# A hybrid two-layer expert kernel on one core: small experts' first stages ahead of big second stages, products during the expert choice, and a twelfth weight slot

## Chip, cores and metric

The kernel runs on one core of one Trainium2 chip. The metric is the device time of one execution in microseconds (us), the median of several runs. All data begins and ends in the chip's memory (HBM).

## What is computed

256 latent rows `x` and 256 context rows `ctx`, 1024 wide in float32, go through two layers. Each layer adds a mixer and then a mixture of experts; only the latent rows leave layer 1. The mixer of layer 0 is a pair of gated convolutions, that of layer 1 is attention beside a pooling group; both end in a product with `w_out`. The part that most of the change concerns is the mixture of experts:

```python
    g_logits = (t @ wg + bg).astype(jnp.float32)
    g_idx = jnp.argmax(g_logits, axis=-1)
...
    top_v, top_i = lax.top_k(e_in, TOP_K)
    top_w = jax.nn.softmax(top_v, axis=-1) * g_w
...
    for e in range(N_EXPERTS):
        hid = jax.nn.silu(t @ w1[e]) * (t @ w3[e])
        out = out + gates[:, e:e + 1] * (hid @ w2[e])
```

Each row chooses one of 4 groups and two of that group's 4 experts; an expert goes from 1024 to 512 columns and back. Its input is a modulated RMS norm of the rows, its output is scaled by a modulation row and added to the rows.

## The kernel before

**Engines.** TensorE does the products, ScalarE and VectorE casts and elementwise work, GpSimd gathers and scatters rows, and the queue of SyncE (SP) issues the weight loads. A scheduler fixes each engine's order when the program is built; `tc.issue_after(i)` holds what it encloses behind instruction i in that order, and `tc.high_priority()` moves it forward. An engine works its list strictly in turn.

**Rows.** `X` holds the 512 rows as four chunks of 128 (0 and 1 latent, 2 and 3 context). Layer 1 ends with the two latent chunks.

**Exact products.** `split` (L85) casts each half of a weight tile to a high part `wh` on ScalarE (L93) and subtracts to get a low part `wl` on VectorE (L94); each has NSPL = 4 buffers. `mm3` (L103) then makes a product of three matmuls, at L105, L106 and L107.

**Mixer's end.** `w_out` (L248) is a generator: it goes through two halves of the columns, and in each through two halves of the depth, four chunks and four products each, adding the result to `X` at L274 and L275. `route_prep` (L436) works out what the router's matrix and bias are with norm gain and modulation folded in; its two small products at L461 spread a bias row `bs` over 128 partitions. `router` (L465) transposes the rows (L481), takes the logits (L484), and `dispatch` chooses groups and experts on VectorE up to a mask `M` (L552). Position products (L557, L559) and a selection of the first expert's rows (`select_rows_T`, L723) follow on TensorE.

**Experts.** `experts` (L904) runs all 16 in an order written by hand:

```python
NBIG = (9, 5)
SEQ = ([0, 1, 9, 2, 10, 3, 11, 4, 12, 5, 13, 6, 7, 14, 8, 15],
       [0, 1, 5, 2, 6, 3, 7, 4, 8, 9, 10, 11, 12, 13, 14, 15])
```

The numbers are ranks: 0 and 1 are experts 0 and 1, the others are looked up in a table worked out at the choice (`number`), so that busier experts have lower ranks. Ranks below NBIG are big (128 row places, exact products with split weights: `ffn_in`, `hidden_T`, `down`), the others small (64 places, plain float32 products straight from the loaded weights: `ffn_in_half` at L808, `hidden_half_T` at L821, `down_half` at L834). Each has a first stage (w1 and w3, four loads), a transposed hidden tile, and a second stage (w2, two loads). The loop issues the first stage of expert i with the hidden transposes of i - 1 between its parts, and then `out_e(i - 1)`: the second stage, weighted rows `y` (L942 in layer 0) and a scatter to `Y` in HBM. Where a small expert follows a big one, `early` splits the big one's w2 tiles during the small first stage.

**Weight slots.** Every expert load is 1 MiB. It goes to one of 7 raw tiles (`wr`) or nx = 4 wide ones (`wx`), eleven in turn, and waits on SyncE's queue until the slot's last reader is through. Eleven loads, up to `(wout, 1, 0)`, are issued ahead of the layer's expert loop (`load_ahead`).

**Layer's end.** The last two experts' rows are not scattered but added by products with a selection matrix `selT` (L1075) and, for the scattered ones, products of the identity with rows loaded from `Y` (L1080 in layer 0, L1084 in layer 1). In layer 0 `add_rows` first adds the two halves of each loaded row on VectorE (L1062), and `rows_out(15)` writes the last rows (L873 on ScalarE, L874 on VectorE). Then `X` is updated at L1094 and L1095.

The functions that the diff touches:

Of the kernel before, what the change touches and what calls it, by code (L numbers as in the profile page):

```python
# [19 lines left out]
KD = 8  # L20
# [24 lines left out]
def backbone(ctx: ExitStack, tc: tile.TileContext, I, out):  # L45
# [57 lines left out]
    def mm3(ps, a, b, start, stop):  # L103
# [3 lines left out]
        return T.matmul(ps, a[0], b[1], start=False, stop=stop)  # L107


    X = cp.tile([128, 4, D], F32, name="X")  # L110
    cols = cp.tile([128, NCOL], F32, name="cols")
# [134 lines left out]
    upd = {}  # L246

    def w_out(W, cat, nch, mrows, pool, khs):  # L248

        def load(h, kh):  # L250
            w = raw()
            nc.sync.dma_start(w.rearrange("p (k n) -> p k n", k=4),
                              W[kh * 512:(kh + 1) * 512, h * 512:(h + 1) * 512].rearrange("(k p) n -> p k n", p=128))
            return split(w)

        seq = [(h, n) for h in range(2) for n in range(2)]
        nxt = load(0, khs[0])
        rows = None
        yield
        for i, (h, n) in enumerate(seq):  # L260
            cur, kh = nxt, khs[n]
            if n == 0:
                ps = [pa() for _ in range(nch)]
            for c in range(nch):
                for k in range(4):
                    mm3(ps[c], [t[:, c * 128:(c + 1) * 128] for t in cat(kh * 4 + k)],
                        cur(k * 512, 512), n == 0 and k == 0, n == 1 and k == 3)
                if i < 3 and c == 0:
                    nxt = load(seq[i + 1][0], khs[seq[i + 1][1]])
                if n == 1:  # L270
                    t = pool.tile([128, 512], F32, name="yt", tag="tmp", bufs=4)
                    if not rows:
                        rows = mrows()
                    V.tensor_tensor(t, ps[c], rows[c // 2][:, h * 512:(h + 1) * 512], op=ALU.mult)  # L274
                    upd[c] = V.tensor_tensor(X[:, c, h * 512:(h + 1) * 512], X[:, c, h * 512:(h + 1) * 512], t, op=ALU.add)  # L275
            yield


    def even_layer():
        with tc.tile_pool(name="ev", bufs=1, reuse_waits="tile") as ep:  # L280
# [147 lines left out]
            while rest:  # L428
                mod_chunk(*rest.pop(0))
            prep = route_prep(0, 2, Ar, Br, ep.tile([128, 2, KD, 32], F32, name="wa", tag="bp"))  # L430
            for _ in wo:
# [4 lines left out]
    def route_prep(l, nr, Ar, Br, wa):  # L436
# [22 lines left out]
        V.tensor_copy(bs[:, 0:nr], pb[0:32, 0, 0:nr])  # L459
        for r in range(nr):  # L460
            T.matmul(pb[:, 2 + r, :], bs[:, r:r + 1].to_broadcast([32, 128]), ident[0:32, 0:32], start=True, stop=True)  # L461
            V.tensor_tensor(bw[:, r, :], pb[:, 2 + r, 0:20], bge[:, l, :], op=ALU.add)
        return Ar, Br, wa, bw

    def router(l, nch, prep):  # L465
# [33 lines left out]
        with tc.high_priority():  # L499
            lgT = sp.tile([128, 128], F32, name="lgT")  # L500
            i = V.tensor_copy(lgT[:32 * nch, :], pl[:32 * nch, :])
            with tc.issue_after(i.ins):
                rows(nch - 1)
            pl2 = py((128, 128))
            T.transpose(pl2[:, :32 * nch], lgT[:32 * nch, :], ident[:32 * nch, :32 * nch])

# [3 lines left out]
    def dispatch(l, nch, nr, pl2, rs, bw, hmD, hms, ir):  # L510
# [44 lines left out]
        for c in range(nch + 1):  # L555
            for cc in range(c):
                T.matmul(pr[:, c], ones_b, M[:, cc], start=cc == 0, stop=c == nch and cc == c - 1)  # L557
            if c < nch:
                T.matmul(pr[:, c], tri, M[:, c], start=c == 0, stop=True)  # L559

# [168 lines left out]
    loaded = []  # L729

    def behind(i):
# [68 lines left out]
    def ffn_in_half(x, loads, hs, between=()):  # L800

        ps = [pa((128, 256)), pa((128, 256))]
        for kh in range(2):
            for m in range(2):
                w = loads.pop(0)()
                for k in range(4):
                    for h in range(2):
                        T.matmul(ps[m][64 * h:64 * h + 64, :], x[:, k, kh * 64:kh * 64 + 64], w[:, k * 512 + h * 256:k * 512 + h * 256 + 256],  # L808
                                 start=kh == 0 and k == 0, stop=kh == 1 and k == 3)
                for f in between[:1]:  # L810
                    f()
                between = between[1:]
# [91 lines left out]
    def experts(l, R, after, mid=None):  # L904
# [3 lines left out]
        with tc.tile_pool(name=f"mp{l}", bufs=1, reuse_waits="tile") as mp:  # L908
# [39 lines left out]
            def out_e(i):  # L948
                rows_out(i, (down_half if small[i] else down)(hT.pop(i), wout[i]))

            win, wout, hs, hT = {}, {}, {}, {}
            nx = 4
            turn = [0]

            def slot():
# [3 lines left out]
                if 2 <= i < NRAW + 2:  # L959
                    return raw()  # L960
                return wide(i % NRAW, [128, 2048])

# [14 lines left out]

            load_ahead([(win, 0, i) for i in range(4)] + [(win, 1, i) for i in range(4)] + [(wout, 0, i) for i in range(2)] + [(wout, 1, 0)])
            if l == 0:
# [75 lines left out]
            def add_rows(c):  # L1055
# [5 lines left out]
                else:  # L1061
                    V.tensor_tensor(y[:, :D], y[:, :D], y[:, D:], op=ALU.add)  # L1062

            for c in range(nch):
                add_rows(c)
            rows_out(NE - 1, po)
            for r in range(R.nr):
# [82 lines left out]
    def odd_layer(A, B):  # L1150
        with tc.tile_pool(name="od", bufs=1, reuse_waits="tile") as op:
# [188 lines left out]
            next(wo)  # L1340
            prep = route_prep(1, 1, ABr[:, 0:1, :], ABr[:, 1:2, :], tmp((128, 2, KD, 32)))
            for _ in wo:
# [119 lines left out]
```

## Time and profile before

| | |
|---|---|
| three runs | 1006.71, 1008.33, 1011.28 us; median 1008.33 |
| profiled execution, its own time | 1006.41 us |
| its span, first to last instruction | 1004.6 us |
| mean granted TensorE clock | 0.966 |
| TensorE busy with matmuls | 915.2 us (91%) |
| VectorE, ScalarE, GpSimd busy | 595.0, 393.7, 124.1 us |
| DMA | 313.66 MB, mean 312 GB/s over the span |
| layer 0: mixer and w_out, choice, experts, end | 0 to 269, to 286, to about 540, to 580 us |
| layer 1: mixer and w_out, choice, experts, finish | 580 to 729, to 742, to 983, to 1004.6 us |

How to read it: the engines run side by side, so their busy times do not add up to the span. What counts is, stage by stage, which wait ends last. A row of the timeline is start, duration, engine, source line, operation, result <- operands, count, and in brackets how long the engine stood before it and on what. A granted clock of 1.00 is TensorE at 2.4 GHz, 0.50 is 1.2 GHz. A float32 matmul appears as two records; `L105`, `L93` and the like are lines of the listing above.

### The profile page before, as it was taken

What the parts mean: (1) busy time and instruction counts of PE and PEld (TensorE: products, weight loads), DVE (VectorE), ACT (ScalarE), POOL (GpSimd) and SP (SyncE); (2) the same over time, 40 slices, a digit from 0 to 9 for tenths busy, and PEclk for the clock granted to TensorE, in tenths of its full rate; (3) what the DMA queues carried; (4) which work ended last, traced back from release to release, by engine and by line L of the source; (5) the groups of instructions that cost most, each with busy time, mean ns of one, the idle gap of its engine ahead of it and who ended that gap; (6) DMA issues with size and microseconds to landing.
All of it is one profiled execution on the core that took longest, in us unless ns stands there. A gap on an engine that the chain in (4) does not pass through costs nothing. (4 is left out here: it accounts for less than half of the span.)

```text
span 1004.6 us, 13295 instructions
## 1 busy us (share of the span) xinstructions
PE 915.2 (91%) x4893; PEld 615.4 (61%) x4893; DVE 595.0 (59%) x942; ACT 393.7 (39%) x571; POOL 124.1 (12%) x127
## 2 busy tenths in 40 slices
PE   2799999999799999999999889999978999999875
PEld 0466776557587776666666368655766766655431
DVE  2689999354778744446544577675587755520004
ACT  2432211321447655445544147433356544411102
POOL 3000000040112111111001011010021211111000
PEclk9899999998999999999999989999978999999999
DMA  9998888993578999999996663253368999999994
GB/s 358 353 335 299 309 320 314 361 343 135 205 307 327 411 407 420 419 399 397 383 355 222 216 226 133 99 191 122 121 227 321 375 388 418 419 418 418 418 419 180
DMA packets 80680, 313.66 MB, mean 312 GB/s; under 512 B 8602, under 2 KB 32154, under 8 KB 50016
## 3 DMA queue, kind: packets, MB, share of 16 engines
q1 hardware_dynamic: 70032, 290.34, 75.0%
q0 software_dynamic: 6368, 11.78, 3.2%
q10 hardware_dynamic: 4208, 10.61, 2.8%
q8 instruction: 40, 0.66, 0.3%
q14 instruction: 32, 0.26, 0.1%
HBM read 301.56 MB, written 21.23 MB: 321 GB/s over the span
## 5 line engine op out<-in xcount | busy, mean ns | idle before, releaser
L93 ACT CAST wh<-wr 128x1024 fp32r<-128x1024 f32 (+2 forms) x170 | 172.0, 1037 | 151.1 <-PE pa L107 50.9
L94 DVE TENSOR_TENSOR wl<-wr,wh 128x1024 fp32r<-128x1024 f32 (+2 forms) x170 | 199.4, 1203 | 53.7 <-ACT wh L93 52.4
L105 PE MATMUL pa<-wh,xh 128*128 128x512 f32 x224 | 93.4, 417 | 6.8 <-ACT wh L93 5.0
L107 PE MATMUL pa<-wl,xh 128*128 128x512 f32 x224 | 91.5, 409 | 2.2 <-DVE wl L94 2.1
L808 PE MATMUL pa<-wr,xs 128*64 128x256 f32 x736 | 88.1, 384 | 4.5 <-DMA wr<-in_moe_w 4.5
L106 PE MATMUL pa<-wh,xl 128*128 128x512 f32 x224 | 90.6, 405 | 0.9 <-DVE xl L712 0.9
L334 DVE SCALAR_TENSOR_TENSOR ca<-apad,cols,ca 128x512 f32<-128x512 f32 x120 | 84.0, 746 | 0.8
L808 PEld LDWEIGHTS pa<-wr,xs 128*64 128x64 f32 x736 | 49.6, 136 | 37.0 <-DMA wr<-in_moe_w 8.2
L105 PE MATMUL pa<-wx,wh 128*128 128x512 f32 x160 | 63.6, 402 | 4.0 <-ACT wx L234 4.0
L106 PE MATMUL pa<-wx,wl 128*128 128x512 f32 x160 | 62.7, 393 | 0.0
L107 PE MATMUL pa<-wx,wh 128*128 128x512 f32 x160 | 62.5, 392 | 0.0
L183 PE MATMUL py<-wr,csil 128*32 128x512 f32 x384 | 51.3, 638 | 11.0 <-ACT csil L154 11.0
L94 DVE TENSOR_TENSOR wl<-wx,wh 128x1024 fp32r<-128x1024 f32 x46 | 54.7, 1221 | 7.0 <-ACT wh L93 5.9
L105 PEld LDWEIGHTS pa<-wh,xh 128*128 128x128 f32 x224 | 43.8, 196 | 17.2 <-ACT wh L93 6.3
L93 ACT CAST wh<-wx 128x1024 fp32r<-128x1024 f32 x46 | 47.0, 1052 | 17.8 <-DVE M L552 6.7
L107 PEld LDWEIGHTS pa<-wl,xh 128*128 128x128 f32 x224 | 43.5, 194 | 14.8 <-DVE wl L94 4.7
L808 PE MATMUL pa<-wx,xs 128*64 128x256 f32 x416 | 49.0, 382 | 2.2 <-DMA wx<-in_moe_w 2.2
L106 PEld LDWEIGHTS pa<-wh,xl 128*128 128x128 f32 x224 | 43.4, 194 | 10.5 <-DVE xl L712 1.2
L815 DVE TENSOR_TENSOR hs<-hs,pa 128x256 f32<-128x256 f32 x18 | 7.6, 422 | 67.9 <-PE pa L808 67.9
L105 PE MATMUL py<-wh,hTh 128*128 128x512 f32 x112 | 46.0, 410 | 1.5 <-ACT wh L93 1.5
L107 PE MATMUL py<-wl,hTh 128*128 128x512 f32 x112 | 44.4, 415 | 2.6 <-DVE wl L94 2.3
L106 PE MATMUL py<-wh,hTl 128*128 128x512 f32 x112 | 44.3, 396 | 0.0
(360 smaller groups left out, 1526.1 us busy)
## 6 DMA issues: line engine op xcount, KB each, us to landing
wr<-in_moe_w SPq DMA_DIRECT2D x124, 1024.0 KB, 12.3
wx<-in_moe_w SPq DMA_DIRECT2D x68, 1024.0 KB, 10.4
wr<-in_w_mod SPq DMA_DIRECT2D x48, 1024.0 KB, 8.5
wr<-in_ev_w_in SPq DMA_DIRECT2D x20, 512.0 KB, 5.9
wr<-Y SPq DMA_DIRECT2D x6, 1024.0 KB, 6.0
wr<-in_ev_w_out SPq DMA_DIRECT2D x4, 1024.0 KB, 5.1
Y<-xg SPq DMA_DIRECT2D x1, 4096.0 KB, 13.3
wr<-in_od_w_out SPq DMA_DIRECT2D x4, 1024.0 KB, 5.1
```

What stands on the lines that cost most here:

```text
L93: S.copy(hi[:, :m], x)
L94: V.tensor_tensor(lo[:, :m], x, hi[:, :m].bitcast(F32), op=ALU.subtract)
L105: T.matmul(ps, a[0], b[0], start=start, stop=False)
L106: T.matmul(ps, a[1], b[0], start=False, stop=False)
L107: return T.matmul(ps, a[0], b[1], start=False, stop=stop)
L183: T.matmul(ps[32 * j:32 * j + 32, :], csil[:, l, k, :], w[:, j * 512:(j + 1) * 512], start=k == 0, stop=k == 7)
L334: V.scalar_tensor_tensor(acc, apad[:, bi, :, t:t + 256], col("caw", t * 4 + bi), acc, op0=ALU.mult, op1=ALU.add)
L808: T.matmul(ps[m][64 * h:64 * h + 64, :], x[:, k, kh * 64:kh * 64 + 64], w[:, k * 512 + h * 256:k * 512 + h * 256 + 256], start=kh == 0 and ...
L815: V.tensor_tensor(hs, hs, ps[1], op=ALU.mult)
```

## The change

It does six things.

1. `route_prep` returns its two bias products as a function `later`. Both layers call it after one more step of `w_out`, behind the last product issued so far (`done[0]`).
2. `awake(i, n)` issues n products of the identity with the router's weights `wge` (128x512) behind an instruction i. Their result is not read. Five (layer 0) or four (layer 1) stand behind the transpose of the logits, one behind the position products.
3. `out_e` issues the second stage of i behind the last first-stage product of i + 1 where expert i + 1 is small (`done[0]`, now also set in `ffn_in_half`).
4. In layer 0 `rows_out(15)` stands behind the last of `add_rows`.
5. `X` becomes two tiles, `xl` (latent) and `xc` (context), with the same index as before.
6. In layer 1 nx is 5: the twelfth slot is the tile `xc`, and one more load, `(wout, 1, 1)`, is issued ahead.

```diff
@@ -106,8 +106,23 @@
         return T.matmul(ps, a[0], b[1], start=False, stop=stop)

-
-    X = cp.tile([128, 4, D], F32, name="X")
+    def awake(i, n):
+
+        with tc.issue_after(i.ins):
+            ps = pa()
+            for _ in range(n):
+                T.matmul(ps, ident, wge.rearrange("p l k n -> p (l k n)"), start=True, stop=True)
+
+
+    class Rows:
+
+        def __init__(self):
+            self.t = [cp.tile([128, 2, D], F32, name=n, tag=n) for n in ("xl", "xc")]
+
+        def __getitem__(self, at):
+            return self.t[at[1] // 2][at[0], at[1] % 2, at[2]]
+
+    X = Rows()
     cols = cp.tile([128, NCOL], F32, name="cols")
     nc.scalar.dma_start(cols, I.cols)
@@ -245,6 +260,8 @@
     upd = {}

+    done = [None]
+
     def w_out(W, cat, nch, mrows, pool, khs):

@@ -263,8 +280,8 @@
             for c in range(nch):
                 for k in range(4):
-                    mm3(ps[c], [t[:, c * 128:(c + 1) * 128] for t in cat(kh * 4 + k)],
-                        cur(k * 512, 512), n == 0 and k == 0, n == 1 and k == 3)
+                    done[0] = mm3(ps[c], [t[:, c * 128:(c + 1) * 128] for t in cat(kh * 4 + k)],
+                                  cur(k * 512, 512), n == 0 and k == 0, n == 1 and k == 3)
                 if i < 3 and c == 0:
                     nxt = load(seq[i + 1][0], khs[seq[i + 1][1]])
@@ -427,7 +444,9 @@
             while rest:
                 mod_chunk(*rest.pop(0))
-            prep = route_prep(0, 2, Ar, Br, ep.tile([128, 2, KD, 32], F32, name="wa", tag="bp"))
+            prep, later = route_prep(0, 2, Ar, Br, ep.tile([128, 2, KD, 32], F32, name="wa", tag="bp"))
+            next(wo)
+            later()
             for _ in wo:
                 pass
@@ -457,10 +476,14 @@
         bs = sp.tile([32, 2], F32, name="bs")
         V.tensor_copy(bs[:, 0:nr], pb[0:32, 0, 0:nr])
-        for r in range(nr):
-            T.matmul(pb[:, 2 + r, :], bs[:, r:r + 1].to_broadcast([32, 128]), ident[0:32, 0:32], start=True, stop=True)
-            V.tensor_tensor(bw[:, r, :], pb[:, 2 + r, 0:20], bge[:, l, :], op=ALU.add)
-        return Ar, Br, wa, bw
+
+        def later():
+            with tc.issue_after(done[0].ins):
+                for r in range(nr):
+                    T.matmul(pb[:, 2 + r, :], bs[:, r:r + 1].to_broadcast([32, 128]), ident[0:32, 0:32], start=True, stop=True)
+                    V.tensor_tensor(bw[:, r, :], pb[:, 2 + r, 0:20], bge[:, l, :], op=ALU.add)
+
+        return (Ar, Br, wa, bw), later

     def router(l, nch, prep):
@@ -502,7 +525,7 @@
                 rows(nch - 1)
             pl2 = py((128, 128))
-            T.transpose(pl2[:, :32 * nch], lgT[:32 * nch, :], ident[:32 * nch, :32 * nch])
+            awake(T.transpose(pl2[:, :32 * nch], lgT[:32 * nch, :], ident[:32 * nch, :32 * nch]), 5 - l)

         with tc.high_priority():
@@ -554,9 +577,10 @@
         for c in range(nch + 1):
             for cc in range(c):
-                T.matmul(pr[:, c], ones_b, M[:, cc], start=cc == 0, stop=c == nch and cc == c - 1)
+                i = T.matmul(pr[:, c], ones_b, M[:, cc], start=cc == 0, stop=c == nch and cc == c - 1)
             if c < nch:
-                T.matmul(pr[:, c], tri, M[:, c], start=c == 0, stop=True)
+                i = T.matmul(pr[:, c], tri, M[:, c], start=c == 0, stop=True)
+        awake(i, 1)

         R.pe = cp.tile([128, nch, 16], F32, name=f"pe{l}", tag="pe")
@@ -805,8 +828,8 @@
                 for k in range(4):
                     for h in range(2):
-                        T.matmul(ps[m][64 * h:64 * h + 64, :], x[:, k, kh * 64:kh * 64 + 64], w[:, k * 512 + h * 256:k * 512 + h * 256 + 256],
-                                 start=kh == 0 and k == 0, stop=kh == 1 and k == 3)
+                        done[0] = T.matmul(ps[m][64 * h:64 * h + 64, :], x[:, k, kh * 64:kh * 64 + 64], w[:, k * 512 + h * 256:k * 512 + h * 256 + 256],
+                                           start=kh == 0 and k == 0, stop=kh == 1 and k == 3)
                 for f in between[:1]:
                     f()
@@ -946,10 +969,13 @@

             def out_e(i):
-                rows_out(i, (down_half if small[i] else down)(hT.pop(i), wout[i]))
+
+                with behind(done[0]) if small[i + 1] else nullcontext():
+                    po = (down_half if small[i] else down)(hT.pop(i), wout[i])
+                rows_out(i, po)

             win, wout, hs, hT = {}, {}, {}, {}
-            nx = 4
+            nx = 4 + l
             turn = [0]

@@ -958,6 +984,9 @@
                 if 2 <= i < NRAW + 2:
                     return raw()
+                if i == NRAW + 4:
+
+                    return cp.tile([128, 2048], F32, name="xc", tag="xc")
                 return wide(i % NRAW, [128, 2048])

@@ -975,7 +1004,7 @@
                     d[e][i] = lambda w=w: w

-            load_ahead([(win, 0, i) for i in range(4)] + [(win, 1, i) for i in range(4)] + [(wout, 0, i) for i in range(2)] + [(wout, 1, 0)])
+            load_ahead([(win, 0, i) for i in range(4)] + [(win, 1, i) for i in range(4)] + [(wout, 0, i) for i in range(2)] + [(wout, 1, 0)] + [(wout, 1, 1)] * l)
             if l == 0:
                 clear(nc.sync, 0, XG[0])
@@ -1059,11 +1088,13 @@
                         V.tensor_tensor(X[:, c, :], X[:, c, :], y[:, h * D:(h + 1) * D], op=ALU.add)
                 else:
-                    V.tensor_tensor(y[:, :D], y[:, :D], y[:, D:], op=ALU.add)
+                    i = V.tensor_tensor(y[:, :D], y[:, :D], y[:, D:], op=ALU.add)
+                    return i

             for c in range(nch):
-                add_rows(c)
-            rows_out(NE - 1, po)
+                i = add_rows(c)
+            with nullcontext() if l else tc.issue_after(i.ins):
+                rows_out(NE - 1, po)
             for r in range(R.nr):
                 cs = (2 * r, 2 * r + 1)
@@ -1338,7 +1369,9 @@
             wo = w_out(I.od_w_out, lambda k: (ch[:, k, :], cl[:, k, :]), 2, lambda: [m2], op, (1, 0))
             next(wo)
-            prep = route_prep(1, 1, ABr[:, 0:1, :], ABr[:, 1:2, :], tmp((128, 2, KD, 32)))
+            prep, later = route_prep(1, 1, ABr[:, 0:1, :], ABr[:, 1:2, :], tmp((128, 2, KD, 32)))
+            next(wo)
+            later()
             for _ in wo:
                 pass
             return router(1, 2, prep)

```

Three places show how the order moves. Line numbers behind the diff's first lines are shifted (L461 becomes L483, L481 L504, L808 L831, L821 L844, L874 L897, L1062 L1091, L1094 L1125).

TensorE, layer 0, in the middle of `w_out` (`pa`: the product's sum, `ah` and `al`: its rows, `bs`: the bias row), before and then after:

```order
L106 MATMUL pa<-wh,al 128x512
L461 MATMUL pt<-ident,bs 128x32
L107 MATMUL pa<-wl,ah 128x512
L105 MATMUL pa<-wh,ah 128x512
L106 MATMUL pa<-wh,al 128x512
L107 MATMUL pa<-wl,ah 128x512
L105 MATMUL pa<-wh,ah 128x512
L461 MATMUL pt<-ident,bs 128x32
L106 MATMUL pa<-wh,al 128x512
L107 MATMUL pa<-wl,ah 128x512
```

```order
L107 MATMUL pa<-wl,ah 128x512
L105 MATMUL pa<-wh,ah 128x512
L106 MATMUL pa<-wh,al 128x512
L504 MATMUL pt<-ident,xl 128x128 x4
L107 MATMUL pa<-wl,ah 128x512
L483 MATMUL pt<-ident,bs 128x32
L105 MATMUL pa<-wh,wx 128x512
L106 MATMUL pa<-wh,wx 128x512
L107 MATMUL pa<-wl,wx 128x512
```

The two products on `bs` stood among the products of the first column half, and the transposes of X behind those; now the transposes come first, one product ahead of the half's end, and the `bs` products stand behind them, the second 12 products further on.

TensorE, layer 0, the fourth pair of a big expert and a small one behind it (`hTh`, `hTl`: the big expert's hidden tile, second stage; `xs`: the small one's rows, first stage; `xh`, `xl`: rows of the next big expert), before and then after:

```order
L107 MATMUL py<-wl,hTh 128x512 x2
L105 MATMUL py<-wh,hTh 128x512
L106 MATMUL py<-wh,hTl 128x512
L808 MATMUL pa<-wr,xs 64x256 x8
L107 MATMUL py<-wl,hTh 128x512
L105 MATMUL py<-wh,hTh 128x512
L106 MATMUL py<-wh,hTl 128x512
L107 MATMUL py<-wl,hTh 128x512
L821 MATMUL pt<-ident,hs 128x128 x2
L699 MATMUL pt<-ident,xg_1961 128x128 x4
L105 MATMUL pa<-wh,xh 128x512
L106 MATMUL pa<-wh,xl 128x512
```

```order
L831 MATMUL pa<-wr,xs 64x256 x8
L802 MATMUL pt<-ident,hs 128x128 x4
L733 MATMUL pt<-ident,xg_1971 128x128 x3
L831 MATMUL pa<-wr,xs 64x256 x8
L733 MATMUL pt<-ident,xg_1971 128x128 x5
L831 MATMUL pa<-wr,xs 64x256 x16
L105 MATMUL py<-wh,hTh 128x512
L106 MATMUL py<-wh,hTl 128x512
L107 MATMUL py<-wl,hTh 128x512
```

Before, the last eight products of the small first stage stand among the second-stage products, the hidden transposes (L821) and those of the gathered rows (L699) next, and the next big expert's first products behind them. After, the whole small first stage stands ahead of all 24 second-stage products; the hidden transposes (L844) come 12 products into the next big expert.

VectorE, end of layer 0 (`xl` at L874 and L897 is the low part of expert 14's rows, `ya` that of expert 15's, `wr` a chunk of the rows loaded from Y, `zt` a scaled sum), before and then after:

```order
L874 SCALAR_TENSOR_TENSOR xl<-py,gate_2095,xh 128x512 x2
L874 SCALAR_TENSOR_TENSOR ya<-py,gate_2095,ya 128x512
L1062 TENSOR_TENSOR wr<-wr 128x1024 x2
L1094 TENSOR_TENSOR zt<-pa,wr 128x512 x2
L1095 TENSOR_TENSOR X<-X,zt 128x512 x2
L1062 TENSOR_TENSOR wr<-wr 128x1024
L1094 TENSOR_TENSOR zt<-pa,wr 128x512
L159 TENSOR_SCALAR rsqm<-ss1b 128x1
L1094 TENSOR_TENSOR zt<-pa,wr 128x512
L223 TENSOR_SCALAR scr<-X,rs1b 128x1024
L1062 TENSOR_TENSOR wr<-wr 128x1024
L1095 TENSOR_TENSOR X<-X,zt 128x512 x2
```

```order
L897 SCALAR_TENSOR_TENSOR xl<-py,gate_2104,xh 128x512 x2
L1091 TENSOR_TENSOR wr<-wr 128x1024 x4
L897 SCALAR_TENSOR_TENSOR ya<-py,gate_2104,ya 128x512
L1125 TENSOR_TENSOR zt<-pa,wr 128x512 x2
L1126 TENSOR_TENSOR xl<-xl,zt 128x512 x2
L1125 TENSOR_TENSOR zt<-pa,wr 128x512 x2
L174 TENSOR_SCALAR rsqm<-ss1b 128x1
```

Before, the last expert's rows stand ahead of all four additions, and two of the additions stand between updates of X. After, all four come first.

## Rows read from the trace of the kernel before

**Rows 1.** Chain of waits, 900 to 1005 us: start us, us, what.
```profile
913.39 6.93 PE pa L808 x64
...
962.93 20.09 DMA wr<-in_moe_w
...
983.16 1.94 PE py L834 x8
```

**Rows 2.** Stretches: length; busy PE, PEld, DVE, ACT, POOL; PEclk, DMA share, GB/s.
```profile
430.00:530.00 100.00, 92.45 (x449) 62.41 (x448) 55.71 (x55) 56.16 (x72) 11.68 (x10) 0.97 0.98 381
...
825.00:985.00 160.00, 148.02 (x951) 86.66 (x949) 46.26 (x54) 38.36 (x57) 21.79 (x19) 1.00 1.01 417
```

**Rows 3.** Timeline of TensorE, w_out of layer 0: start us, us, instruction [idle before].
```profile
225.38 0.40 PE L461 MATMUL pt<-ident,bs 32*128 32x32 f32 x2 [2.24 <-DVE bs L459]
...
230.05 0.63 PE L106 MATMUL pa<-wh,al 128*128 128x512 f32 x1
230.48 0.63 PE L107 MATMUL pa<-wl,ah 128*128 128x512 f32 x1
...
233.57 0.39 PE L107 MATMUL pa<-wl,ah 128*128 128x512 f32 x1
233.80 0.60 PE L481 MATMUL pt<-ident,X 128*128 128x128 f32 x4
```

**Rows 4.** Timeline of VectorE, w_out of layer 0.
```profile
225.25 1.20 DVE L94 TENSOR_TENSOR wl<-wr,wh 128x1024 fp32r<-128x1024 f32 x1
...
228.81 1.28 DVE L274 TENSOR_TENSOR yt<-pa,wr 128x512 f32<-128x512 f32 x2
230.00 1.28 DVE L275 TENSOR_TENSOR X<-X,yt 128x512 f32<-128x512 f32 x2
```

**Rows 5.** Timeline of TensorE: choice of layer 0, of layer 1, and the end.
```profile
275.28 0.19 PE L559 MATMUL py<-M,tri 128*128 128x16 bf16 x1 [5.64 <-DVE M L552]
...
276.86 9.12 PE L723 MATMUL pt<-scr 128*128 128x128 f32 x64 [1.04 <-DVE scr L566]
...
734.17 0.20 PE L559 MATMUL py<-M,tri 128*128 128x16 bf16 x1 [4.91 <-DVE M L552]
...
735.22 6.70 PE L723 MATMUL pt<-scr 128*128 128x128 f32 x32 [0.74 <-DVE scr L566]
...
991.75 3.70 PE L1084 MATMUL pa<-wr,ident 128*128 128x512 f32 x8 [0.34 <-DMA wr<-Y]
```

**Rows 6.** Stretches at the two choices, columns as in rows 2.
```profile
277.00:280.50 3.50, 3.50 (x17) 3.50 (x18) 3.50 (x18) 0.32 (x2) 0.00 (x0) 0.51 1.01 406
735.00:741.00 6.00, 5.78 (x27) 5.78 (x28) 5.27 (x17) 3.17 (x7) 2.79 (x2) 0.50 0.33 138
741.00:744.00 3.00, 3.00 (x17) 2.60 (x17) 1.90 (x12) 2.02 (x3) 0.00 (x0) 0.96 0.37 87
```

**Rows 7.** Waits of TensorE, 425 to 560 us: total us, times, longest.
```profile
PE pa L105 <- ACT wh L93: 4.4, 4, 1.7
PE py L107 <- DVE wl L94: 2.3, 1, 2.3
PE pa L107 <- DVE wl L94: 2.1, 4, 0.5
PE py L105 <- ACT wh L93: 1.2, 4, 0.3
```

**Rows 8.** Waits of TensorE, 290 to 425 us.
```profile
PE py L105 <- ACT wh L93: 0.3, 1, 0.3
```

**Rows 9.** Timeline of ScalarE, 420 to 440 us.
```profile
429.65 1.40 ACT L942 ACTIVATE y<-py,gate 128x512 f32<-128x512 f32 x2 [3.90 <-PE py L107]
```

**Rows 10.** Timelines of VectorE, then TensorE, end of layer 0.
```profile
565.76 0.75 DVE L874 SCALAR_TENSOR_TENSOR ya<-py,gate,ya 128x512 fp32r<-128x512 f32 x1 [5.40 <-ACT ya L873]
566.43 2.35 DVE L1062 TENSOR_TENSOR wr<-wr 128x1024 f32<-128x1024 f32 x2
...
567.70 1.98 PE L1080 MATMUL pa<-wr,ident 128*128 128x512 f32 x4 [2.04 <-DVE wr L1062]
```

## Prediction

> **What bounds the kernel now.** I read the chain of waits first, from its end. Its last long steps are weight loads, the last of them 20.09 us from issue to landing with others in flight, and TensorE's next products begin where it lands [rows 1]. The table by stretches says why: from 825 to 985 us the DMA engines are busy throughout at 417 GB/s, while TensorE works for 148 of 160 us [rows 2]. So the end of layer 1 is set by how many loads are still to come, and by when the slots for them came free. From 430 to 530 us, in layer 0, the DMA engines look almost as busy (0.98), but their rate is 381 GB/s. The waits of TensorE from 425 to 560 us name the casts of the split weights, ScalarE's high halves and VectorE's low ones, and no DMA [rows 2, 7]. So there time is lost in TensorE's own chain. Whatever shortens that chain ahead of 825 us frees slots earlier and moves the later loads with it. Three more places of that chain are waits around the router and the layer's end; each has its part below.
>
> **Constant products of the route.** In layer 0 TensorE stands 2.24 us for the bias row bs before the two products at L461, then runs at half clock (1.2 of 2.4 GHz): its products start 0.43 us apart (230.05, 230.48), later 0.23 (233.57, 233.80) [rows 3]. The change sends 18 products ahead of that point and the constant products behind them. TensorE is free at 225.38 - 2.24 = 223.14; 19 products at 0.23 bring it to 227.5. There the transposes of X wait in turn: VectorE still does two low halves at 1.20, two yt products in 1.28 and the first of two X additions at 0.64 [rows 4], from 225.25 to 229.6. They start there and not at 233.80, 4.2 us earlier. But 2.1 us of that is a new wait, nearly as long as the old one, and the old one cost much of the clock: 225.38 to 233.80 is 8.42 us for 19 products, which at 0.23 take 4.4; of the 4.0 more I put 1.0 on the constant products themselves and 3.0 on the clock. If the new wait costs as much, 1.2 is left; if nothing, 4.2. I take **2.2**: the clock falls, but shorter, since the wait is. In layer 1 I found no wait at this product: nothing.
>
> **Products that keep TensorE awake.** At the choice TensorE stands 5.64 us in layer 0 and 4.91 in layer 1 [rows 5], and the select products that follow begin at half clock (0.51 in layer 0 until 280.5, 0.50 in layer 1 until 741) [rows 6]. The change puts 5 and 4 products of the 128x128 identity with 512 columns there. The same form at L1084 takes 3.70 us for 8 records, which are 4 instructions: 0.925 us each [rows 5]. That is 4.6 us in a wait of 5.64, and 3.7 in one of 4.91, so they end 1 us early and cost nothing. One more follows the position products, 0.925 in waits of 1.04 and 0.74, so 0.2 late in layer 1. If the clock holds, the stretch from 276.86 to 280.5 halves: 1.8 us. VectorE, busy for all of 277 to 280.5 with the choice's own work [rows 6], caps that; I take **1.5** of 0 to 1.8. In layer 1 about 6 us at half clock would give 3.0, but VectorE's idle time is only 0.73 + 1.10 us there [rows 6]; I take **1.8** of 0 to 3.0 (nothing, if the clock falls anyway).
>
> **Second stages behind the next first stage.** In layer 0 the big expert's down products alternate with the next, small expert's first stage from the fourth such pair on. Behind them ScalarE has two weighted rows of 0.70 us [rows 9] and a hidden copy ahead of the next big expert's casts, and TensorE waits for those casts. The change puts the small first stage ahead, so that the big down products cover what ScalarE owes. Of the waits in rows 7, 4.4 + 2.1 + 2.3 + 1.2 = 10.0 us, two (2.2 together: the longest of 1.7 and one of 0.5 behind it) fall between two big experts and stay. At most 7.8 us go, at four transitions; one in layer 1 changes too. Nothing less than zero is to be expected of the new order alone: the first three transitions already have it, and from 290 to 425 us the casts of weights cost TensorE 0.3 us in all [rows 8]. The DMA engines limit the gain: 100 us at 381 GB/s would be 91 at 417 [rows 2], 9 us of room, but not at every transition. I take **6.0** of 0 to 7.8. What the old order covered, and the new doesn't, is a late load of the small first stage: the down products stood between its parts (third rival).
>
> **Last rows behind the additions.** At layer 0's end VectorE stands 5.40 us for ScalarE's last row (L873), and only then adds the Y halves at L1062, two of which take 2.35. TensorE waits 2.04 for them [rows 10]. Behind the change all four additions run inside the 5.40 us (4.7, if Y has landed), so the 2.04 goes, and the third and fourth, 1.18 each, leave the X chain. That is 2.0 to 4.4; I take **3.5**, since the odd layer's start also waits for other things.
>
> **A twelfth slot.** X is split, so the context's half can take one MiB load in layer 1. It is issued on SyncE's queue behind the band load, with nothing to wait for but the last reader of the context's rows. One load fewer is left for the saturated stretch: 1.0486 MB at 417 GB/s [rows 2], **2.5** us, all of it on the path, as TensorE has 12 us of slack there. The Trainium skill, "DMA: Bandwidth & Descriptors", section "Specifications", gives about 358 GB/s as a core's HBM limit. By that the load would be worth 2.9 us and the sum 0.4 more; the row shows 417, so the measurement stands.
>
> **Sum.** 2.2 + 1.5 + 1.8 + 6.0 + 3.5 + 2.5 = 17.5 us off the profiled execution's 1006.41, so 988.9. The median of the three runs, 1008.33, is 1.9 above that execution, so **990.8 us**. All lower ends (1.2, 0, 0, 0, 2.0, 2.5) give 5.7 us and 1002.6; all upper ends (4.2, 1.8, 3.0, 7.8, 4.4, 2.5) 23.7 and 984.6.
>
> **Rivals.**
> First, the load stream already binds in layer 0: the 6.0 of the second stages is absorbed, and the new wait at the transposes costs the full half clock. What is left is 1.2 + 1.5 + 1.8 + 3.5 + 2.5 = 10.5, so 997.8. For it speaks the share near 1 there, against it that no wait there names a DMA [rows 2, 7].
> Second, the clock falls at the choice all the same: the products end about 1 us before the mask, and single short waits remain. Then 3.3 us are lost: 994.1. For it: a wait of 2.24 us was enough to lose the clock in rows 3; against it, no gap here is that long. The Trainium skill, "TensorE: Matmul & The Clock Gate", section "A second HAM failure mode: psum-queue depth-cycling", tells of short idle gaps between groups that make the clock oscillate; no run here shows it at this place.
> Third, slower: at the five changed transitions the small first stage now stands whole ahead of the down products, and its four loads are late. TensorE runs such a stage in 6.93 us [rows 1], four loads at 2.5 us are 10.0, so it waits 3.1 where the down products, 24 at 0.23 or 5.5 us, used to fill in, and the clock falls (up to 3.0 as above, middle 1.5): 4.6. Five are 23.0, against 11.5 from the other parts: 11.5 slower, **1019.8**. It decides from the third such transition on. Against it: no wait in rows 7 names a DMA, so the loads are ahead there, by up to eleven slots.
> Fourth, the twelfth slot does nothing, because its load waits for the context's last reader and delays the loads queued behind it: 2.5 lost, 993.3. Against it: the loads near 600 us are few.
>
> **How the numbers follow.** Forecast 0.52, first rival 0.18, second 0.14, fourth 0.10, third 0.06. The range of 8 in 10 runs from 984 to 1002, about the two ends of the sum: it holds the first, second and fourth rival, and leaves out the third and misses that add up. 0.5% is 5 us, about what a measurement here can tell from no change, so faster means under 1003.3. The forecast and the three mild rivals lie there, 0.94, less 0.06 for misses that add up: 0.88. Slower by over 0.5% is the third rival, less a little: 0.05. The rest, 0.07, is the same.
>
> **What would show it.** In layer 0 the 2.24 us wait at the constant products is gone, and the first transposes of X wait about 2 us and start 4 us earlier against the w_out stage's beginning. The select products take about 7.3 and 4 us (9.12 and 6.70 before [rows 5]) at a granted clock of 1.0. The sum of cast waits between 425 and 545 us falls from 10 to some 2 to 4. The 2.04 us wait at L1080, now L1111, is gone. The last weight load lands about 16 us earlier, and the stretch before it still shows a DMA share near 1. I'd be wrong if waits for loads of 2 us or more stand at the small first stages of layer 0, if the choice still shows 0.50, or if the last load lands less than 8 us earlier although TensorE reaches layer 1 earlier.

## The result and the profile after

The changed kernel took 991.33 us (988.52 to 993.46, 4 runs) against 1008.96 beside it: ratio 0.9841, 95% interval 0.9818 to 0.9863. The forecast was 990.8. Two later measurements of the same kernel gave 0.9810 (0.9779 to 0.9840) and 0.9811 (0.9786 to 0.9835).

The page of the changed kernel's profiled execution (988.52 us), as against a span of 1004.6 us before:

```profile
span 986.8 us, 13346 instructions
...
PE 910.4 (92%) x4915; PEld 615.9 (62%) x4915; DVE 595.9 (60%) x942; ACT 393.7 (40%) x571; POOL 122.0 (12%) x127
```

TensorE is busy 4.8 us less than the 915.2 before, although eleven awake products of 0.925 us came in.

The chain of waits at its end, then the stretch from 800 us (length; busy PE, PEld, DVE, ACT, POOL; PEclk, DMA share, GB/s):

```profile
944.11 20.07 DMA wx<-in_moe_w
...
964.31 1.94 PE py L857 x8
```

```profile
800.00:965.00 165.00, 154.36 (x994) 92.56 (x992) 48.80 (x57) 41.59 (x61) 23.52 (x20) 1.00 1.01 418
```

The last load still ends the chain [rows 1], in a stream as full as before [rows 2], and lands 18.8 us earlier (944.11 + 20.07 = 964.18, against 983.02). So what happened ahead of it was passed on. Where it happened shows when layer 0's late part is cut at the starts of the small experts' second stages (L834, now L857). The work between two starts is the same, as the counts show. Before, then after, in the columns above:

```profile
410.11:446.05 35.94, 33.78 (x172) 21.81 (x171) 17.35 (x17) 17.10 (x22) 4.82 (x4) 0.95 1.01 412
446.05:480.79 34.74, 33.33 (x176) 21.22 (x175) 16.99 (x17) 16.46 (x21) 4.84 (x4) 1.00 1.00 392
480.79:537.46 56.67, 52.33 (x251) 36.11 (x250) 33.73 (x33) 32.48 (x41) 4.07 (x4) 0.97 0.94 358
537.46:560.29 22.83, 19.99 (x114) 10.93 (x113) 8.50 (x11) 6.96 (x10) 3.80 (x5) 1.00 0.51 183
```

```profile
412.38:442.70 30.32, 30.32 (x172) 21.26 (x171) 16.99 (x17) 16.93 (x22) 4.81 (x4) 1.00 1.02 420
442.70:473.49 30.79, 30.79 (x176) 21.74 (x175) 17.08 (x17) 16.41 (x21) 4.35 (x4) 1.00 1.01 419
473.49:523.26 49.77, 48.68 (x251) 35.51 (x250) 33.46 (x33) 32.11 (x41) 4.79 (x4) 1.00 1.01 413
523.26:544.86 21.60, 18.70 (x114) 11.36 (x113) 8.40 (x12) 7.06 (x10) 3.79 (x5) 1.00 0.71 280
```

The four stretches together went from 150.18 to 132.48 us: 17.70 less, as much as the whole gain (they start 2.3 us later, and what follows them is 2.4 us shorter). 6.76 of it are waits (stretch less busy PE: 10.75 before, 3.99 after). The other 10.94 are TensorE's own busy time for the same instructions. Part of that is the clock, at 0.95 and 0.97 in the first and third stretch before, 1.00 after; by the granted clocks of their slices of 2 us, an estimate, it cost 3.4 us. The larger part is not the clock: in the second and fourth stretch the clock was 1.00 both times, and still the busy time fell by 2.54 and 1.29. Taken apart by the starts of its products, with the waits taken off, the second stretch became shorter by 1.1 us in the 24 second-stage products, by 0.9 in the transposes of the gathered rows, and by 0.7 in the small experts' products and the hidden transposes; the next big expert's 48 first-stage products took 11.5 us both times.

TensorE's waits for casts from 425 to 560 us, 10.0 in rows 7, are now these (total us, times, longest):

```profile
PE py L107 <- DVE wl L94: 2.7, 1, 2.7
PE pa L105 <- ACT wh L93: 0.6, 1, 0.6
...
PE pa L107 <- DVE wl L94: 0.5, 1, 0.5
```

That is 3.8. The one long wait for low halves stayed, 2.3 before and 2.7 now; of the two that were to stay (2.2) half went.

The places of the other parts. The constant products, TensorE's timeline:

```profile
231.83 0.63 PE L504 MATMUL pt<-ident,xl 128*128 128x128 f32 x4 [1.73 <-DVE xl L292]
...
232.62 0.40 PE L483 MATMUL pt<-ident,bs 32*128 32x32 f32 x2
```

The old wait of 2.24 is gone and the new one is 1.73 [rows 3]. The clock stays at 1.00 here.

The choice, layer 0 and then layer 1:

```profile
268.87 4.46 PE L114 MATMUL pa<-wge,ident 128*128 128x512 f32 x10
274.68 0.18 PE L582 MATMUL py<-M,tri 128*128 128x16 bf16 x1 [1.35 <-DVE M L575]
...
276.24 7.41 PE L747 MATMUL pt<-scr 128*128 128x128 f32 x64
283.40 0.48 PE L105 MATMUL pa<-wh,xh 128*128 128x512 f32 x1
```

```profile
713.25 3.70 PE L114 MATMUL pa<-wge,ident 128*128 128x512 f32 x8
718.23 0.18 PE L582 MATMUL py<-M,tri 128*128 128x16 bf16 x1 [1.28 <-DVE M L575]
...
719.31 3.79 PE L747 MATMUL pt<-scr 128*128 128x128 f32 x32
```

The awake products (L114) fill the waits of 5.64 and 4.91 up to 1.35 and 1.28, and the select products take 7.41 and 3.79 us for 9.12 and 6.70 [rows 5]. In this profile that part does, up to here, what was forecast. In the changed kernel's two later profiles the clock fell at layer 0's choice all the same. The same stretch there, 276 to 278 us, in the first profile and then in the second:

```profile
276.00:278.00 2.00, 1.92 (x16) 1.77 (x16) 2.00 (x10) 0.32 (x2) 0.00 (x0) 1.00 1.02 410
```

```profile
276.00:278.00 2.00, 2.00 (x11) 2.00 (x11) 2.00 (x10) 0.00 (x0) 0.00 (x0) 0.50 1.02 410
```

The end of layer 0:

```profile
549.71 3.60 PE L1111 MATMUL pa<-wr,ident 128*128 128x512 f32 x8
...
564.53 0.69 PE L1147 MATMUL pt<-ident,scr 128*128 128x128 f32 x2 [2.64 <-DVE scr L238]
```

The products on the rows from Y start without a wait, where 2.04 stood [rows 10], but the second transposes of layer 1, the odd layer, now wait 2.64 us for VectorE, where they waited 0.51 before.

### The profile page after: what moved, and what is told of

Its sections match the earlier page's. It is cut to its first block, busy times and chain, and to the rows that moved or that the text cites. A ratio compares the mean times of both kernels' runs of the same rounds, so it can differ in the third digit from the quotient of the medians.

```text
span 986.8 us, 13346 instructions
## 1 busy us (share of the span) xinstructions
PE 910.4 (92%) x4915; PEld 615.9 (62%) x4915; DVE 595.9 (60%) x942; ACT 393.7 (40%) x571; POOL 122.0 (12%) x127
## 5 line engine op out<-in xcount | busy, mean ns | idle before, releaser
L94 DVE TENSOR_TENSOR wl<-wr,wh 128x1024 fp32r<-128x1024 f32 (+2 forms) x168 | 197.2, 1204 | 42.7 <-ACT wh L93 41.2
L831 PE MATMUL pa<-wr,xs 128*64 128x256 f32 x640 | 75.6, 383 | 4.0 <-DMA wr<-in_moe_w 4.0
L831 PEld LDWEIGHTS pa<-wr,xs 128*64 128x64 f32 x640 | 43.7, 137 | 30.8 <-DMA wr<-in_moe_w 7.9
L831 PE MATMUL pa<-wx,xs 128*64 128x256 f32 x416 | 49.5, 382 | 1.8 <-DMA wx<-in_moe_w 1.8
L105 PE MATMUL pa<-wh,wx 128*128 128x512 f32 (+1 forms) x112 | 42.8, 384 | 0.5 <-ACT wh L93 0.5
```

The source lines that it names most:

```text
L94: V.tensor_tensor(lo[:, :m], x, hi[:, :m].bitcast(F32), op=ALU.subtract)
L105: T.matmul(ps, a[0], b[0], start=start, stop=False)
L831: done[0] = T.matmul(ps[m][64 * h:64 * h + 64, :], x[:, k, kh * 64:kh * 64 + 64], w[:, k * 512 + h * 256:k * 512 + h * 256 + 256], start=k ...
```

## The experiments

Each ratio is against the kernel before, measured beside it on the same chip; the changed kernel itself came out at 0.984, 0.981 and 0.981 in three measurements.

**The second stages alone.** Every other part is taken back, except that X stays two tiles and that in layer 1 the constant products keep their new place:

```diff
-            with nullcontext() if l else tc.issue_after(i.ins):
+            with nullcontext():
                 rows_out(NE - 1, po)
-            nx = 4 + l
+            nx = 4
...
-            next(wo)
-            later()
+            later(False)
...
-            awake(T.transpose(...), 5 - l)
+            awake(T.transpose(...), 0)
...
-        awake(i, 1)
```

> Only the second stages are moved behind the next first stage; the constant products, the awake products, the order at layer 0's end and the eleven slots are as before (X stays split in two tiles). Theory: this part is most of the change. In the two traces the five late transitions of layer 0 took 5.6, 4.0, 2.8, 4.1 and 1.2 us less, 17.7 together, so this kernel is 13 to 18 us faster than before, 991 to 996. Rival, the size in my prediction: 6 us, about 1003.

Measured 991.91 us, 0.9855 (0.9823 to 0.9887): 14.6 us off by the ratio. This part is most of the change. The split of X was not tried by itself. The constant products of layer 1 gain nothing: from its first router product to the logits' transpose it is 29.3 to 29.4 us in the profile before and in all the others.

**All but the second stages.**

```diff
-                with behind(done[0]) if small[i + 1] else nullcontext():
+                with nullcontext():
                     po = (down_half if small[i] else down)(hT.pop(i), wout[i])
```

> The changed kernel with the second stages issued where they were before. Theory: it loses nearly the whole gain, 1004 to 1009. Rival, the size in my prediction: 6 us are lost, about 997. In both cases the waits for casts between 425 and 560 us should be back, some 8 to 10 us.

Measured 1004.72 us, 0.9978 (0.9955 to 1.0001). The other five parts together are worth some 2 us, between none and 4.5 by the interval, where the forecast had 11.5. The waits of TensorE from 400 to 560 us (total us, times, longest), of this kernel and then of the one with the second stages alone:

```profile
PE pa L105 <- ACT wh L93: 4.4, 4, 1.7
PE py L105 <- ACT wh L93: 2.8, 5, 1.6
PE pa L107 <- DVE wl L94: 2.1, 4, 0.5
PE py L107 <- DVE wl L94: 2.1, 1, 2.1
```

```profile
PE py L107 <- DVE wl L94: 2.2, 1, 2.2
PE pa L105 <- ACT wh L93: 0.6, 1, 0.6
PE pa L107 <- DVE wl L94: 0.5, 1, 0.5
```

The cast waits are back with the old order, 11.4 us in all (one of 1.6 ahead of 425 us), and 3.3 without it.

**Layer 0's awake products left out, twice, and both layers'.**

```diff
-            awake(T.transpose(...), 5 - l)
+            awake(T.transpose(...), 4 * l)
...
-        awake(i, 1)
+        if l:
+            awake(i, 1)
```

> The changed kernel without the six awake products of layer 0. Theory: TensorE comes 2.3 us earlier out of the choice with them, but stands for the gathered rows of the second expert until 300 us all the same, and loses the clock in that longer wait; without them the select products take 9.1 us again and the kernel is 0 to 2.5 us faster, 989 to 991.5. Rival, the size in my prediction: 1.5 us slower, 993.

> Layer 0's awake products left out, a second time, now beside the changed kernel. Theory: what they gain at the choice (1.5 us) is given back behind it, since the earlier start meets waits for the second expert's rows and casts (1.39 and 0.93 us for 0.44 and 0.87) that cost the clock: the same or up to 2 us faster than the changed kernel. Rival, the size in my prediction: 1.5 us slower. Should it be 3.5 us or more faster again, the products cost something that the traces have not shown.

> The awake products of both layers left out. Theory: in layer 1 they bring the first expert's products forward by 2.9 us and the second expert's by 1.2; the load stream passes about that on, so this is 1 to 2 us slower than the kernel without layer 0's alone. Rival: the saturated stream behind absorbs it, the same.

Measured 985.57 us, 0.9775 (0.9735 to 0.9814), then, beside the changed kernel, 987.12, 0.9806 (0.9775 to 0.9837) against its 0.9811; without both layers' 986.31, 0.9794 (0.9769 to 0.9819). No part of the awake products can be measured as a gain. The traces show where the time goes. In layer 0 the clock held at the choice in four of the eight profiles with the products and fell in the other four, behind the same waits; it fell in all six without. The first expert's first product comes 14.7 us behind the logits' transpose where it held, 16.3 where it fell, and 16.1 to 17.4 without the products. In layer 1 it held in all eleven profiles with them and fell in the three without. What was gained is then lost at the next wait. With them (the changed kernel's second profile) the second expert's rows meet these waits, and the stretch behind them runs at half clock; without layer 0's, the waits are the shorter ones of the last listing:

```profile
297.62 1.21 PE L733 MATMUL pt<-ident,xg 128*128 128x128 f32 x8 [0.99 <-DVEq L904]
300.21 0.50 PE L105 MATMUL pa<-wh,xh 128*128 128x512 f32 x1 [1.39 <-ACT xh L735]
301.64 0.50 PE L105 MATMUL pa<-wh,xh 128*128 128x512 f32 x1 [0.93 <-ACT wh L93]
```

```profile
303.00:305.00 2.00, 2.00 (x6) 1.60 (x5) 1.90 (x3) 1.04 (x1) 0.00 (x0) 0.50 0.25 100
```

```profile
298.44 1.21 PE L736 MATMUL pt<-ident,xg 128*128 128x128 f32 x8 [1.00 <-DVEq L907]
300.08 0.50 PE L105 MATMUL pa<-wh,xh 128*128 128x512 f32 x1 [0.44 <-ACT xh L738]
301.46 0.49 PE L106 MATMUL pa<-wh,xl 128*128 128x512 f32 x1 [0.87 <-DVE xl L739]
```

From the logits' transpose to the first small second stage, layer 0 takes 80.3 to 84.6 us in eight profiles with the products, and 79.2 to 79.6 in five of six without (83.2 in the other, where the clock also fell). The clock fell behind the second expert's rows in all eight profiles with them. In layer 1 the second expert's rows come 25.8 to 27.3 us behind the transpose with them, and 26.0 to 27.0 without: the first expert starts 1.4 to 2.9 us earlier and then waits. The first small second stage there begins 77.5 to 78.7 us behind the transpose in eleven profiles with them, and at 76.7 and 76.9 in the two without that have the moved second stages. So up to there the products cost about a microsecond or more in both layers, that one profile aside, and gain nothing.

**Awake products in those waits too.**

```diff
+            if l == 0:
+                keep(3)
             x = list(tokens_T(1))[1]
+            keep(1)
```

`keep(n)` issues the same products as `awake`, at that place.

> The changed kernel with three more awake products ahead of the transposes of the second expert's gathered rows in layer 0, and one behind those transposes in both layers, so that TensorE works in the waits there. Theory: the half clock behind these waits (301 to 308 us in layer 0, 741 to 748 in layer 1 of the changed kernel) is what the early arrival costs, about 2 to 3.5 us in each layer: 985 to 988. Rival: what follows is set by the casts or by the loads, and nothing is gained: 990 to 992, with the clock at 1.0 in both stretches.

Measured 985.79 us, 0.9778 (0.9742 to 0.9813). That overlaps the changed kernel's intervals, and in its profile the clock fell all the same, in layer 0 from 303.5 to 306.5 us, behind a wait of 1.45 for VectorE's low rows, and in layer 1 from 743 to 747 us, behind one of 2.76 for the high rows. Whether a kernel that keeps the clock there is faster stays open.

**The changed kernel again.**

> The changed kernel once more, without an edit, so that the three below and the two before stand against it on equal terms. If the 5.8 us by which the kernel without layer 0's awake products came out ahead of it are the products' doing, it is at 0.984 of before (990 to 992) again. If they are scatter between jobs, it is at 0.978 to 0.980.

> The changed kernel a third time, as the measure of the three below: 0.981 to 0.984 of before.

Measured 986.71 us, 0.9810 (0.9779 to 0.9840), and 988.72, 0.9811 (0.9786 to 0.9835). So 3 us of the 5.8 that seemed to separate it from the kernel without layer 0's awake products were scatter between measurements.

**The constant products at their old place in layer 0.**

```diff
-            next(wo)
-            later()
+            later(False)
```

> The changed kernel with the constant products of layer 0 at their old place. Theory: at the transpose of the logits this part gained at most 2 us, and what follows (the wait for the second expert's rows until 300 us) takes it in part: 0 to 2 us slower than the changed kernel. Rival, the size in my prediction: 2.2 us slower; and if the new wait at the transposes cost as much as the old one: the same.

Measured 988.48 us, 0.9828 (0.9799 to 0.9856), beside 0.9810 for the changed kernel: 1.8 us, within the intervals. Its profile has a wait of 1.51 for bs, and here the clock did not fall:

```profile
226.93 0.40 PE L482 MATMUL pt<-ident,bs 32*128 32x32 f32 x2 [1.51 <-DVE bs L477]
...
232.30 0.60 PE L503 MATMUL pt<-ident,xl 128*128 128x128 f32 x4
```

```profile
228.00:230.00 2.00, 2.00 (x10) 1.38 (x10) 2.00 (x6) 0.00 (x0) 0.00 (x0) 1.00 0.02 8
```

From the first router product (L457, L476 after) to the logits' transpose it is 46.5 us here, 46.9 to 47.4 in ten profiles with the change, 50.3 in the profile before and 48.2 in the second-stages kernel, where the clock fell. In one profile with the change (both awake parts out) the new wait was 2.17 and the clock fell too, for 50.4:

```profile
230.60:238.00 7.40, 7.38 (x21) 5.57 (x21) 4.19 (x7) 0.00 (x0) 0.00 (x0) 0.55 0.30 125
```

So the part was worth 3.4 us in one profile where the old wait lost the clock, 1.3 in the other, and nothing where it didn't; and its own wait can lose the clock too.

**The old order at layer 0's end.**

```diff
-            with nullcontext() if l else tc.issue_after(i.ins):
+            with nullcontext():
                 rows_out(NE - 1, po)
```

> The changed kernel with the last expert's rows of layer 0 ahead of the scheduler's own place for the additions, as before. Theory: in the traces the products on the loaded rows came 2.6 us earlier by this part, but the transposes of the odd layer only 0.6 to 1.4 us earlier: 0.5 to 1.5 us slower. Rival, the size in my prediction: 3.5 us slower.

Measured 985.52 us, 0.9789 (0.9760 to 0.9817) beside 0.9810: no gain of this part shows in the time. Its timeline:

```profile
548.35 3.60 PE L1111 MATMUL pa<-wr,ident 128*128 128x512 f32 x8
...
564.09 0.44 PE L1147 MATMUL pt<-ident,scr 128*128 128x128 f32 x2 [3.04 <-DVE scr L238]
```

The products on the rows from Y have no wait here either. With the second stages moved the scheduler had already put two of the four additions ahead of the last rows, here and in the kernel with the second stages alone, as this piece of VectorE's order shows:

```
L897 SCALAR_TENSOR_TENSOR xl<-py,gate,xh 128x512 x2
L1091 TENSOR_TENSOR wr<-wr 128x1024 x2
L897 SCALAR_TENSOR_TENSOR ya<-py,gate,ya 128x512
```

The odd layer's second transposes wait 3.04 us for VectorE here, and 2.64 in the changed kernel. Read between marks the part gains 0.9 us: from the last small second stage to these transposes it is 20.6 us here and in the kernel with the second stages alone, and 19.7 in the changed kernel's first two profiles. With the second stages at their old place it gains 0.7 (21.1 in the kernel before, 20.4).

**Eleven slots.**

```diff
-            nx = 4 + l
+            nx = 4
...
- + [(wout, 1, 1)] * l)
+)
```

> The changed kernel with eleven slots in layer 1 and no load into the context's half. Theory: the last load ends one load's time later, 2.5 us slower, with the stretch from 825 us at 417 to 419 GB/s in both. Rival: the stream is not full between the choice and 800 us, so a load more or less ahead shifts nothing at the end: the same.

Measured 989.04 us, 0.9841 (0.9810 to 0.9871) beside 986.71, 0.9810: 2.3 us slower, as the theory has it, but the intervals overlap. The spans of single profiles can't show 2.5 us here: the stretch of layer 1 ahead of its experts, from the first transposes to the first router product, took 120.1 to 125.6 us. From the logits' transpose of layer 1 to the landing of the last load it is 250.6 to 252.6 us in eleven profiles with twelve slots, and 252.2, 253.1 (this kernel) and 254.0 in three with eleven: 1.8 us between the means, with an overlap.

**One wait more taken out.** VectorE's second shuffle for layer 1 is held behind the last small expert's hidden rows; layer 0's awake products are out as well:

```diff
         for g in (1, 2):
-            shuffle(1, g)
+            with tc.issue_after(split_done[0].ins) if g == 2 else nullcontext():
+                shuffle(1, g)
```

`split_done[0]` is VectorE's multiplication that ends the hidden rows in `ffn_in_half`.

> The kernel without layer 0's awake products, and with layer 1's second shuffle of the modulation rows held on VectorE behind the last small expert's hidden rows. Theory: VectorE stands 7.5 us for GpSimd's broadcast (the rows' last reader) ahead of the last big expert's low halves, and TensorE waits 2.6 to 3.5 us for those at the last transition of layer 0: 2 to 3 us faster than the kernel without layer 0's awake products. Rival: the rows loaded from Y are late next, and the layer ends where it did: the same.

Measured 983.79 us, 0.9754 (0.9727 to 0.9780), clear of the changed kernel's 0.9811 (0.9786 to 0.9835) beside it, and 3.3 us under the same kernel without this edit (intervals just overlap). The changed kernel's second profile has VectorE's stand for GpSimd ahead of the shuffle, the shuffle, the low halves behind it, and on TensorE the wait for them:

```profile
537.08 0.01 DVE L189 LOAD_MASK_SELECT modc<-modr  x1 [7.54 <-POOL wr L229]
537.08 0.72 DVE L189 STREAM_SHUFFLE modc<-modr 128x512 f32<-128x512 f32 x1
537.69 2.35 DVE L94 TENSOR_TENSOR wl<-wr,wh 128x1024 fp32r<-128x1024 f32 x2
```

```profile
538.96 0.50 PE L107 MATMUL py<-wl,hTh 128*128 128x512 f32 x1 [2.59 <-DVE wl L94]
```

In the kernel without layer 0's awake products that wait is 1.98 and 3.46 us in its two profiles. In the edited kernel none is left from 400 to 560 us; its longest wait and its two waits for casts there are:

```profile
PE pt L1151 <- DVE scr L240: 2.6, 1, 2.6
PE pa L105 <- ACT wh L93: 0.6, 1, 0.6
...
PE pa L107 <- DVE wl L94: 0.5, 1, 0.5
```

From layer 0's first small second stage to the odd layer's first transposes it takes 207.4 us, against 209.2 and 213.4 without the edit: 1.8 us less than the better of the two, near the 2 to 3 expected. This is the fastest version of the study.

## Why the prediction was right, and where it was not

The time was right, and so was the account of what bounds the kernel: loads end the chain, and what is gained ahead of them is passed on. But that the sum came out is luck: it had 8.6 us too little for the second stages and some 9 too much for the other five terms, and the two errors cancel.

**Second stages, 6.0 forecast, 14.6 measured alone.** The direction and the place were right; the term was mis-sized at "At most 7.8 us go". That bound took the waits of rows 7 for all that the old order cost. The waits went as forecast, from 10.0 to 3.8, and were 6.76 us of the 17.70. The rest was inside TensorE's busy time: the half clock behind the waits, which I had priced in the first part and not here (3.4 us, an estimate), and time in which the alternating products took longer at full clock, 2.5 us in the second stretch and 1.3 in the fourth. What makes them longer (the weight loads at each change between the two kinds of product, short waits that the list does not show, or the change itself) was not tried apart. The cap by the DMA rate, 9 us of room, did not hold: the first three stretches are 16.5 us shorter. They now run at 413 to 420 GB/s instead of 358 to 412, about as fast as layer 1's full stream (417 to 418), and part of the loads moved on into the fourth (280, where it was 183). The first rival, that the load stream absorbs this gain, did not come.

**Awake products, 3.3 forecast, nothing measurable.** Two steps failed. The clock held at layer 1's choice, but at layer 0's only in half of the profiles, so the second rival came true there half the time. And where the clock held, the next wait took the gain: I asked whether VectorE would cap the gain at the choice, and not what the first expert's end waits for. It is the second expert's gathered rows and their casts (1.39 and 0.93 us above, and 3.47 and 3.03 ahead of the rows' transposes in the changed kernel's other two profiles). What is late next was named for other parts and not for this one. Some 25 us behind the choice of layer 0 the clock fell in every profile with the products.

**Last rows, 3.5 forecast, nothing measurable in the time, 0.9 between marks.** The wait of 2.04 did go, but it goes without this part too. The failing step is that the order of VectorE was taken from the whole change and credited to one edit, and that nearly all of it was taken to reach the odd layer's start, which now waits for VectorE instead.

**Constant products, 2.2 forecast, 1.8 measured without certainty.** The new wait came as forecast (1.73 for 2.1), with the clock held, not lost.

**Twelfth slot, 2.5 forecast, 2.3 measured without certainty, 1.8 at the last load's landing.** Its price rested on the rate of the stream, 417 to 418 GB/s before and after. The figure of the Trainium skill ("DMA: Bandwidth & Descriptors", "Specifications"), about 358, is not what this core was held to.

The third rival, late loads at the small first stages, came only in its beginnings. No such wait stands in the changed kernel's three profiles from 400 to 560 us. But in seven of the twelve profiles with the second stages moved, the last small first stage of layer 0 waits for a load, 0.4 to 1.2 us in six and 2.50 in the kernel with awake products in the waits. That is over the 2 us that I had named as the sign of being wrong, at one place and not at every transition, and that kernel was not slower. The fourth rival did not show.

## What to carry to other kernels

Cut a stretch at the same instruction in two kernels and compare the busy time of equal work: what alternation or a half clock costs is in no list of waits. Before a gain at one place is put into a sum, ask for each part by itself what the engine waits for next, and read more than one profile before a clock is said to hold. Terms that come from one scheduler's order should be undone one at a time before any of them is believed.

## What the runs showed of the hardware

The clock is not settled by the order alone. At layer 0's choice, with the awake products in place, it fell in four profiles and held in four behind the same wait of 1.35 us. In layer 0's w_out, waits of 2.24 and 1.73 us for bs were followed by half clock and one of 1.51 was not; a wait of 2.17 at the transposes of X was followed by half clock, and one of 2.22 at the same place and those of 1.7 were not. Further on, at the second expert's rows, it fell after waits of 1.39 and 0.93, and after 0.44 and 0.87 it held in five profiles and fell in one. The longer pair stands in five profiles with layer 0's awake products and in none without them; what sets that was not tried apart. And the first 220 us, where all kernels do the same, differ by 3 us between profiled executions (the first router product starts at 218.8 to 221.8), so a part worth 2 us is read from stretches between marks or from many runs, not from two spans.
